# Issuing a small first load from ScalarE's queue, beside the first large load, in a DMA-bound pooling kernel

## The chip, the cores and the metric

The kernel runs on one core of one Trainium2 chip. The metric is the device time of one execution in microseconds (us); medians of several executions are quoted with their range. A trace also gives the span, from the first to the last recorded event, which is 1.8 us shorter than the time in most kernels here. "SP" and "ACT" are the two queues that issue transfers; both feed the same 16 DMA engines: in the trace of the kernel before, the packets of both (3,501 and 1,053) lie on the same 16 strings, one for each engine. ACT (ScalarE) and DVE (VectorE) also do the arithmetic. "Row" means the contiguous piece that one DMA engine moves as one packet into one partition (the 19 large loads into 128 partitions are 2,432 packets of 52,736 bytes).

## The reference

Average pooling with p = 2: squares are summed over windows of four, divided by four, and the square root is taken.

```python
x: (32, 256, 4096) float32, p = 2.0, kernel_size = 4
window = np.abs(x[:, :, 4*i : 4*i+4]) ** p
result[:, :, i] = np.mean(window, axis=-1) ** (1.0 / p)     # (32, 256, 1024)
```

So 134.22 MB are read and 33.55 MB written, with little arithmetic for each byte.

## The kernel before

The input is cut into 20 pieces of 128 partitions, most of them 13,184 columns wide (52,736 bytes in each partition), which go through three buffers. ACT squares a piece in place, DVE sums groups of four, ACT takes the root, and a store follows for every two pieces. 840 columns' worth of elements (430 KB) do not fit this pattern: the "odd" piece. It is viewed as 30 rows of 3,584 elements and borrows part of the second output buffer.

```python
def load(i):
    ...
    nc.sync.dma_start(out=v, in_=block(xf, g, 1)[:, src:src + w])
...
Q = 30
odd = ODD * P // Q                      # 3,584 elements
t = o_tiles[1][0:Q, 0:odd]
nc.sync.dma_start(out=t, in_=xf[(total - ODD) * P:total * P].rearrange("(p w) -> p w", p=Q))
ahead = 0
while ahead < n and loads[ahead][0] < X_SLOTS:      # three large loads at once
    load(ahead)
    ahead += 1
nc.vector.tensor_tensor(out=t, in0=t, in1=t, op=mybir.AluOpType.mult)
o = o_tiles[1][0:Q, odd:odd + odd // k]
nc.vector.tensor_reduce(out=o, in_=t.rearrange("p (n j) -> p n j", j=k), ...)
nc.scalar.activation(out=o, in_=o, func=Act.Sqrt, scale=1.0 / k)
stores["odd"] = nc.scalar.dma_start(out=of[...], in_=o)
for i in range(n):                      # the large pieces
    ...                                 # load(s) into a free buffer, Square, sum, root, store
```

## Time and profile before

| | before |
|---|---|
| median of the first three runs | 394.82 us (393.62 to 395.62) |
| span of the profiled run | 393.3 us |
| DVE, ACT busy | 70%, 70% |
| DMA engines, both queues | 99% |
| bytes moved | 167.77 MB at 427 GB/s |

The lines that carry this stand in the prediction. Two more views are needed. The first is the page's list of transfers: what is written from what, queue, operation and count, size of each, us from issue to landing.

```profile
xt<-in_x_dram SPq DMA_DIRECT2D x19, 6592.0 KB, 31.6
ot<-in_x_dram SPq DMA_DIRECT2D x1, 420.0 KB, 4.2
out_dram<-ot ACTq DMA_DIRECT2D x1, 105.0 KB, 8.7
```

The small load, alone at the start, lands after 4.2 us. The second is the timeline: the squares of the second and third large piece begin when these pieces have landed, within half a microsecond (start, duration, engine, line, operation, and in brackets the idle time and what ended it).

```profile
36.18 11.19 ACT L167 ACTIVATE xt<-xt 128x13184 f32<-128x13184 f32 x1 [4.39 <-DMA xt<-in_x_dram]
51.76 11.19 ACT L167 ACTIVATE xt<-xt 128x13184 f32<-128x13184 f32 x1 [4.39 <-DMA xt<-in_x_dram]
```

Third, a tool: the single packets of the trace. Each has a start, a duration, a queue and a size, but no engine number. Each large load ends with a 4-byte packet on each of its engines; the times of these 16 packets tell when the first, the middle and the last engine finished that load. In the kernel before, the third load was done at 50.73, 51.19 and 51.34 us; its 16 semaphore events follow 0.4 to 0.5 us later, from 51.13 to 51.82 on the same count. All packet times here, those of the prediction included, count from a moment some 0.08 us ahead of the zero of the timeline; differences between packets are not touched by that.

### The profile page before, as it was taken

Reading aid. Unit: us, or ns where it says so; the run is one execution under the profiler, and the core shown is the slowest. Engines: PE = TensorE matmul, PEld = TensorE weight load, DVE = VectorE, ACT = ScalarE, POOL = GpSimd, SP = SyncE. Lnnn points to the kernel's source line nnn. Section 1 sums busy time; section 2 is a strip of 40 time slices with the busy share of each in tenths; the row PEclk is TensorE's granted clock in tenths of the full one; section 3 lists DMA queues with packets and bytes.
Section 4 is the critical chain, followed back from the end, with each engine's and each line's share of the span. In section 5 each row is a group of like instructions: output and inputs, shape, how many; then the busy total and the mean of one; then the engine's idle time right before and its main releaser. Section 6 shows DMA issues by size and latency. Waiting matters only on the chain.

```text
span 393.3 us, 182 instructions
## 1 busy us (share of the span) xinstructions
DVE 274.5 (70%) x36; ACT 275.4 (70%) x38; POOL 0.2 (0%) x4
## 2 busy tenths in 40 slices
DVE  4207898885869376948693869396929690989991
ACT  1095879919990899099809991998099809986991
POOL 0000000000000000000000000000000000000000
DMA  8999999999989999999999999999999899999996
GB/s 312 429 440 429 467 445 451 381 432 469 434 386 429 472 429 429 456 402 429 429 432 426 429 472 429 456 400 467 429 437 429 386 429 467 429 429 423 440 409 295
DMA packets 4554, 167.77 MB, mean 427 GB/s; under 512 B 526, under 2 KB 526, under 8 KB 556
## 3 DMA queue, kind: packets, MB, share of 16 engines
q1 hardware_dynamic: 3501, 144.04, 85.0%
q10 hardware_dynamic: 1053, 23.73, 14.0%
HBM read 134.22 MB, written 33.55 MB: 427 GB/s over the span
## 4 chain that ended last, share of the span: by engine, by line
DMA 54%; ACT 25%; DVE 19%; SPq 0%; issue 0%; ACTq 0%
DMA xt<-in_x_dram 54%; ACT xt L167 22%; DVE ot L111 14%; DVE xt L122 3%; ACT ot L102 3%; DVE ot L124 1%; DVE xt L124 1%; ACT xt L102 1%; SPq L82 0%; ACTq L99 0%; SPq L132 0%
## 5 line engine op out<-in xcount | busy, mean ns | idle before, releaser
L167 ACT ACTIVATE xt<-xt 128x13184 f32<-128x13184 f32 (+4 forms) x23 | 217.4, 9458 | 97.9 <-DMA xt<-in_x_dram 96.2
L111 DVE TENSOR_REDUCE ot<-xt 128x3296 f32<-128x13184 f32 x15 | 208.3, 13886 | 88.7 <-ACT xt L167 88.7
L102 ACT ACTIVATE ot<-ot 128x6592 f32<-128x6592 f32 x9 | 51.1, 5679 | 0.0
L122 DVE TENSOR_TENSOR xt<-xt 128x3296 f32<-128x3296 f32 (+5 forms) x9 | 34.5, 3834 | 16.9 <-ACT xt L167 16.8
L124 DVE TENSOR_TENSOR ot<-xt 128x3296 f32<-128x3296 f32 (+1 forms) x4 | 10.9, 2733 | 0.1
L143 ACT ACTIVATE ot<-ot 30x896 f32<-30x896 f32 x1 | 0.9, 948 | 10.8 <-DVE ot L139 10.8
L137 DVE TENSOR_TENSOR ot<-ot 30x3584 f32<-30x3584 f32 x1 | 3.9, 3880 | 5.0 <-DMA ot<-in_x_dram 5.0
L124 DVE TENSOR_TENSOR xt<-xt 128x1448 f32<-128x1448 f32 (+4 forms) x5 | 7.0, 1409 | 0.2
L102 ACT ACTIVATE xt<-xt 128x3296 f32<-128x3296 f32 (+3 forms) x4 | 5.8, 1445 | 1.1 <-DVE xt L124 1.1
L164 DVE TENSOR_TENSOR xt<-xt 128x5792 f32<-128x5792 f32 x1 | 6.2, 6184 | 0.0
L139 DVE TENSOR_REDUCE ot<-ot 30x896 f32<-30x3584 f32 x1 | 3.9, 3874 | 0.0
L143 ACT ACT_TABLE_LOAD x1 | 1.3, 1283 | 0.7 <-PEq L200 0.7
L200 POOL MEMSET const-bfloat16-1.0<- 128x1 bf16 x1 | 0.1, 101 | 0.0
L200 POOL MEMSET const-uint8-127<- 128x1 uint8 x1 | 0.1, 101 | 0.0
L200 POOL MEMSET const-float32-0.0<- 128x1 f32 x1 | 0.1, 98 | 0.2 <-issue 0.2
L200 POOL MEMSET const-float32-1.0<- 128x1 f32 x1 | 0.1, 98 | 0.0
## 6 DMA issues: line engine op xcount, KB each, us to landing
xt<-in_x_dram SPq DMA_DIRECT2D x19, 6592.0 KB, 31.6
out_dram<-ot ACTq DMA_DIRECT2D x7, 3296.0 KB, 27.4
out_dram<-ot SPq DMA_DIRECT2D x2, 3296.0 KB, 24.0
xt<-in_x_dram SPq DMA_DIRECT2D x1, 5404.0 KB, 24.1
out_dram<-xt SPq DMA_DIRECT2D x1, 1648.0 KB, 11.0
out_dram<-xt SPq DMA_DIRECT2D x1, 1351.0 KB, 6.6
ot<-in_x_dram SPq DMA_DIRECT2D x1, 420.0 KB, 4.2
out_dram<-ot ACTq DMA_DIRECT2D x1, 105.0 KB, 8.7
```

What stands on the lines that cost most here:

```text
L102: r = nc.scalar.activation(out=o, in_=o, func=Act.Sqrt, scale=1.0 / k)
L111: r = nc.vector.tensor_reduce(out=o, in_=v.rearrange("p (n j) -> p n j", j=k), axis=mybir.AxisListType.X, op=add,)
L122: r = nc.vector.tensor_tensor(out=h, in0=q[:, :, 0:2], in1=q[:, :, 2:4], op=add)
L124: r = nc.vector.tensor_tensor(out=o, in0=h[:, :, 0], in1=h[:, :, 1], op=add)
L137: nc.vector.tensor_tensor(out=t, in0=t, in1=t, op=mybir.AluOpType.mult)
L139: nc.vector.tensor_reduce(out=o, in_=t.rearrange("p (n j) -> p n j", j=k), axis=mybir.AxisListType.X, op=mybir.AluOpType.add,)
L143: nc.scalar.activation(out=o, in_=o, func=Act.Sqrt, scale=1.0 / k)
L164: r = nc.vector.tensor_tensor(out=v, in0=v, in1=v, op=mybir.AluOpType.mult)
L167: r = nc.scalar.activation(out=v, in_=v, func=Act.Square)
L200: nc = _bacc.Bacc("TRN2", target_bir_lowering=False, num_devices=1)
```

## The change

SP takes about half a microsecond for the small load (an issue of 0.45 us and a gap of 0.06) before it issues the first large one at 1.24 us. The change gives the small issue to ACT's queue, so that both start at once. Nothing else moves.

```diff
-    nc.sync.dma_start(out=t, in_=xf[(total - ODD) * P:total * P].rearrange("(p w) -> p w", p=Q))
+    nc.scalar.dma_start(out=t, in_=xf[(total - ODD) * P:total * P].rearrange("(p w) -> p w", p=Q))
```

## The prediction

The sum: it came to -0.51 us at best and 0 at worst, taken as -0.3, so 394.82 - 0.3 = 394.5 us.

> **What bounds the kernel now.** I read the head of the page first, to see whether an engine or the transfers are full.
>
> ```profile
> DVE 274.5 (70%) x36; ACT 275.4 (70%) x38; POOL 0.2 (0%) x4
> DMA packets 4554, 167.77 MB, mean 427 GB/s; under 512 B 526, under 2 KB 526, under 8 KB 556
> q1 hardware_dynamic: 3501, 144.04, 85.0%
> q10 hardware_dynamic: 1053, 23.73, 14.0%
> DMA xt<-in_x_dram 54%; ACT xt L167 22%; DVE ot L111 14%; DVE xt L122 3%; ACT ot L102 3%; DVE ot L124 1%; DVE xt L124 1%; ACT xt L102 1%; SPq L82 0%; ACTq L99 0%; SPq L132 0%
> ```
>
> The two compute engines are busy 70%. The packets of the two queues take 85.0 + 14.0 = 99% of the time of the 16 DMA engines, so the kernel is bound by moving 167.77 MB. The chain that ended last (the last line) names compute for 46%, but that is a path through buffer releases: while ACT and DVE work, loads issued earlier keep the DMA engines full. A cheaper or earlier compute step is worth nothing unless it lets a DMA engine start earlier, end earlier, or not run dry.
>
> Second, the busy time by stretches, at the two ends and in the middle. Columns: stretch, its length, busy us of DVE, ACT and POOL with instruction counts, clock, DMA share, GB/s. (A packet is booked whole where it falls, so short stretches overshoot 1.)
>
> ```profile
> 0.00:1.00 1.00, 0.00 (x0) 0.27 (x1) 0.20 (x4) 1.00 0.00 0
> 1.00:2.00 1.00, 0.00 (x0) 1.00 (x1) 0.00 (x0) 1.00 0.70 186
> 60.00:360.00 300.00, 215.73 (x23) 218.58 (x26) 0.00 (x0) 1.00 1.00 434
> 388.00:390.00 2.00, 0.00 (x0) 0.00 (x0) 0.00 (x0) 1.00 1.01 428
> 390.00:392.00 2.00, 0.00 (x0) 0.00 (x0) 0.00 (x0) 1.00 0.14 59
> ```
>
> The middle runs at share 1.00 and 434 GB/s: nothing to win. The DMA is idle only in the first 2 us and the last 3. The change touches the first 2.
>
> Third, the timeline of the start.
>
> ```profile
> 0.73 1.28 ACT L143 ACT_TABLE_LOAD   x1 [0.73 <-PEq L200]
> 0.73 0.45 SPq L132 DMA_DIRECT2D ot<-in_x_dram  x1
> 1.24 44.83 SPq L82 DMA_DIRECT2D xt<-in_x_dram  x4
> 4.96 3.88 DVE L137 TENSOR_TENSOR ot<-ot 30x3584 f32<-30x3584 f32 x1 [4.96 <-DMA ot<-in_x_dram]
> 8.88 3.87 DVE L139 TENSOR_REDUCE ot<-ot 30x896 f32<-30x3584 f32 x1
> 12.78 0.95 ACT L143 ACTIVATE ot<-ot 30x896 f32<-30x896 f32 x1 [10.77 <-DVE ot L139]
> 13.76 0.64 ACTq L144 DMA_DIRECT2D out_dram<-ot  x1
> 20.60 11.19 ACT L167 ACTIVATE xt<-xt 128x13184 f32<-128x13184 f32 x1 [6.87 <-DMA xt<-in_x_dram]
> ```
>
> SP needs 0.45 us to issue the small load and starts the first large one at 1.24. That 1.24 - 0.73 = 0.51 us is all that the change can take off SP. The small piece is off the path: it is done at 14.40, while ACT's first square waits for the large load until 20.60.
>
> Fourth, I followed the single packets of the trace by engine (each packet starts some 3 ns before the one ahead of it on its engine ends, so 16 strings can be told apart). Fifteen of them carry two 14,336-byte rows of the small load, start at 1.81 to 2.34 us, and go on with a 52,736-byte row of the large load at 3.2 to 4.0 without a gap. The sixteenth has no part of the small piece: its first packet, a large row, starts at 2.94, which is 1.70 after SP began that issue. From then on no string shows a gap. At the end the fifteen finish at 390.3 to 390.7 and **the sixteenth at 392.17**, though it moved 35,848 bytes less. Four large-row stretches explain it: its rows normally take 1.947 us, but two near 70 us took 2.22 and 2.77, and four between 304 and 325 us took 2.18 to 2.37, some 2.3 us lost in all. So what sets the end in this execution is the one engine whose start the change can bring forward.
>
> [...] what can be saved is the 0.51 us above, and the strings are shared by both queues. [...] the trace shows 30 rows on 15 strings, two each. [...] the small store of 105 KB, issued on ACT's queue beside a running large load, takes 8.7 us to land, against 4.2 for the small load that goes first; its rows start at 17.59 to 20.03, after one or two large rows of 1.95 us each. [...]
>
> **The change part by part.**
> Removed: one issue of 0.45 us plus 0.06 gap from SP's queue, on the path to the first large packet. Effect if nothing takes its place: SP begins the large load at 0.73, the sixteenth engine's first packet at 0.73 + 1.70 = 2.43 instead of 2.94, and its end moves from 392.17 to 391.66: **-0.51 us**. It stays the last (the others end by 390.7 and move the same bytes).
> Added: one issue of about 0.45 us on ACT's queue at 0.73, ahead of the table load of 1.28 us. The table load then ends near 2.5; its first user is the square root of the small piece, not before 12.78. **Cost 0.**
> Moved: the small load now shares each of fifteen engines with a large load. These engines have the same bytes to move from the same earliest start (1.8), so their end does not change: **0**, perhaps plus 0.1 to 0.4 if their first packet comes later, still inside their slack of 392.17 - 390.7 = 1.5 us.
> Moved with it: the small piece's own chain. Taking the small store's 8.7 us as an estimate for a small transfer between large rows, it lands at 0.73 + 8.7 = 9.4 instead of 4.96. Then 3.88 + 3.87 on DVE and 0.95 on ACT, with some 0.1 of hand-over, end at 18.2, and the store's issue of 0.64 at 18.9. The first square comes at 20.60, so 1.7 us are left: **0**. Were it to overrun, the first square and through it the release of the first buffer would slip; the fourth large load goes out at 46.07 - 0.33 = 45.7, while the third's last rows end at 51.34, and with 1.7 us from issue to packet some 3.9 us are still to spare before an engine would run dry.
> The small store moves later by about 4.5 us, with the same bytes. The next user of that output buffer is the second pair's reduction after 60 us: 0.
> Sum: -0.51 us at best as worked out, 0 at worst that I think likely. I take half to most of it: **-0.3**, so 394.82 - 0.3 = 394.5.
>
> **The rivals.** (a) *The full half microsecond*: both issues run side by side at 0.73 and the sixteenth engine is the last again. For it: the end of the strings. It gives 394.3. [...] (c) *The last engine is another one*: the six long rows of the sixteenth engine may be accidents of that execution. Without them it would end at about 389.9, ahead of the fifteen, and then a start half a microsecond earlier buys nothing: 394.8. For it: the long rows come in two clusters. Against: all other engines have only one or none beyond their first row, and it is unlikely that chance picks just the one engine without a small piece. (d) *Harm by taking turns*: the small piece lands so late behind large rows that ACT[...] begins the first square late, and the buffer release with it. It needs a landing later than 11.1 us to touch the square and later than about 15 to starve an engine; that would make 395.5 to 398. Two large rows ahead of each of its two rows would be 4 x 1.95 = 7.8 us after 2, so 9.8: against it. (e) *More than half a microsecond*: the first rows are slow (the first large rows take 2.3 to 2.8 us instead of 1.95, the small ones 0.6 to 1.1 against the 0.53 that 14,336 bytes take at the large rows' rate). Beginning both together might hide some of this; up to 1 us, 393.8.
>
> **Range and chances.** The mechanism spans 393.8 to 394.8 with a tail to 396. The three times of the kernel before spread over 2.0 us (393.62 to 395.62), larger than the effect; a median of three on each side moves by some 0.7 us. Together about 1.2 us either way for 8 in 10: **393.3 to 395.7 around 394.5**. Two per cent is 7.9 us; the idle DMA time at both ends is only some 5 us together, so faster by over 2% is all but impossible (0.005), and slower by over 2% needs an engine to run dry several times (0.01). Within 2%: 0.985.
>
> **What would show it.** Right: in the timeline SP's first large issue starts at 0.73 and ACT's small one too, each of 0.35 to 0.5 us; the sixteenth string's first packet is near 2.43; the small piece's DVE work starts between 7 and 10 us; the first square still at 20.0 to 20.7; DMA share 1.00 in the middle; the whole ends 0.3 to 0.5 us earlier, with the sixteenth string last. [...] Rival (c): another string is last. Wrong altogether: the first square later than 21.5, a gap in the strings near 50 us, a new wait in the list of waits that names a store or a small load, or a middle stretch under 430 GB/s.

## The result

| | before | changed |
|---|---|---|
| median of 6 runs each, same rounds | 394.45 us (393.62 to 395.62) | 395.91 us (395.55 to 396.20) |
| ratio | | 1.0032, 95% interval 1.0011 to 1.0053 |
| span of the profiled run | 393.3 us | 394.0 us |

A ratio in this document compares two kernels in the same rounds; it stays within 0.0003 of the ratio of their mean times and is not quite that of the medians quoted. The change is within 2%, as predicted, but it made the kernel slower by 0.3%, and 395.91 lies above the predicted range (393.3 to 395.7).

The page of the changed kernel, same lines as in the prediction (engines, packets, the two queues, the chain that ended last):

```profile
DVE 274.5 (70%) x36; ACT 275.4 (70%) x38; POOL 0.2 (0%) x4
DMA packets 4554, 167.77 MB, mean 426 GB/s; under 512 B 526, under 2 KB 526, under 8 KB 556
q1 hardware_dynamic: 3456, 143.61, 84.9%
q10 hardware_dynamic: 1098, 24.16, 14.3%
DMA xt<-in_x_dram 50%; ACT xt L167 25%; DVE ot L111 14%; DVE xt L122 3%; ACT ot L102 3%; DVE ot L124 1%; DVE xt L124 1%; ACT xt L102 1%; ACTq L99 0%; SPq L82 0%
```

The 45 packets and 0.43 MB of the small load have moved from SP's queue (q1) to ACT's (q10). Work, bytes and packets are the same, and so is the share of 99% (85.0 + 14.0 before, 84.9 + 14.3 now). So the engines were not idle longer; they took longer for the same bytes. The timeline says when:

```profile
0.73 95.70 SPq L82 DMA_DIRECT2D xt<-in_x_dram  x7
0.74 0.65 ACTq L132 DMA_DIRECT2D ot<-in_x_dram  x1
1.42 1.28 ACT L143 ACT_TABLE_LOAD   x1 [1.42 <-PEq L200]
12.57 3.88 DVE L137 TENSOR_TENSOR ot<-ot 30x3584 f32<-30x3584 f32 x1 [12.57 <-DMA ot<-in_x_dram]
20.39 0.95 ACT L143 ACTIVATE ot<-ot 30x896 f32<-30x896 f32 x1 [17.69 <-DVE ot L139]
22.31 11.19 ACT L167 ACTIVATE xt<-xt 128x13184 f32<-128x13184 f32 x1 [0.97 <-DMA xt<-in_x_dram]
38.16 11.19 ACT L167 ACTIVATE xt<-xt 128x13184 f32<-128x13184 f32 x1 [4.66 <-DMA xt<-in_x_dram]
53.75 11.19 ACT L167 ACTIVATE xt<-xt 128x13184 f32<-128x13184 f32 x1 [4.40 <-DMA xt<-in_x_dram]
```

The first square starts at 22.31 instead of 20.60, the third at 53.75 instead of 51.76. Each was released by the large load, not by the small piece, whose root was done at 21.34. The loss of 2 us is complete by the time the second square starts. The rates of the first 10 us agree (stretch, length, busy time of DVE, ACT, POOL, clock, DMA share, GB/s; a packet is booked whole, so such short stretches are rough). Before:

```profile
2.00:12.00 10.00, 7.00 (x2) 0.01 (x1) 0.00 (x0) 1.00 1.10 436
```

Changed:

```profile
2.00:12.00 10.00, 0.00 (x0) 0.70 (x1) 0.00 (x0) 1.00 0.91 307
```

The packets say what was slow. A row of 52,736 bytes normally takes 1.947 us. In the kernel before, 17 such rows that start in the first 16 us take over 2.1 us: the first large row of each engine, and a second one on one engine. In the changed kernel it is 48, the first three of each of the 16 engines, at 2.2 to 3.6 us, while the small rows pass between them. One of these engines has no small row at all, and its rows are as slow (2.65, 2.90 and 2.89 us). Per engine:

| mean over the engines, us lost against full rate | before | changed |
|---|---|---|
| large rows of the first 16 us, over 1.947 us each | 0.55 | 2.31 |
| two small rows, over the 0.53 us that 14,336 bytes take at that rate | 2 x (0.87 - 0.53) = 0.68 | 2 x (0.73 - 0.53) = 0.40 |
| sum | 1.23 | 2.71 |
| third load done on the middle engine | 51.19 us | 52.65 us |

The sums differ by 1.48 us, the landings of the third load by 1.46. So the start accounts for the delay of the middle engine, and that delay lasts: 1.36 us at 301 us, where a later load lands on the middle engine at 300.44 before and 301.80 changed. The two spans differ by only 0.7 us because in the trace of before one engine loses another 1.3 us on four slow rows after 304 us and ends 1.5 us behind the others.

### The profile page after: what moved, and what is told of

Its sections match the earlier page's. It is cut to its first block, busy times and chain, and to the rows that moved or that the text cites. A ratio compares the mean times of both kernels' runs of the same rounds, so it can differ in the third digit from the quotient of the medians.

```text
span 394.0 us, 182 instructions
## 1 busy us (share of the span) xinstructions
DVE 274.5 (70%) x36; ACT 275.4 (70%) x38; POOL 0.2 (0%) x4
## 3 DMA queue, kind: packets, MB, share of 16 engines
q1 hardware_dynamic: 3456, 143.61, 84.9%
q10 hardware_dynamic: 1098, 24.16, 14.3%
## 4 chain that ended last, share of the span: by engine, by line
DMA 50%; ACT 28%; DVE 19%; another core or an unknown queue 1%; issue 0%; ACTq 0%; SPq 0%
DMA xt<-in_x_dram 50%; ACT xt L167 25%; DVE ot L111 14%; DVE xt L122 3%; ACT ot L102 3%; DVE ot L124 1%; DVE xt L124 1%; ACT xt L102 1%; ACTq L99 0%; SPq L82 0%
## 6 DMA issues: line engine op xcount, KB each, us to landing
ot<-in_x_dram ACTq DMA_DIRECT2D x1, 420.0 KB, 11.8
```

## The experiments

Two theories were on the table first. **Turns:** an engine that alternates between two queues which both load loses time at each turn. **Start:** the engines are slow for their first 10 us, whatever comes. A third came with them. **Place:** the 30 rows go to partitions 0 to 29, the large rows to all 128; what counts is to which partitions the small rows are written. "Crowding" below is short for the slow large rows (2.2 to 3.6 us in the changed kernel) that go with small rows in the low partitions. This theory stood as a guess until the runs below. The prediction had counted the engines that take part (15), and had not asked to which partitions they write.

All kernels gave right results unless it is said otherwise. Medians of before differ between the sets of runs (394.06, 393.92, 395.00, 394.55 us), so the ratios are what compares. The runs came in four sets, each on one chip, with before in the same rounds. The times of before fall into two groups, about 393.7 to 394.1 and 394.9 to 395.5 us, and the share of the slower group differs: it is 8 of 11 runs in the set of the 60-row versions and 4 or 2 of 11 in the two sets ahead of it, which makes the ratios of the 60-row versions look better. In the versions that move the root behind the first square, or compute the small piece in two halves, the time exceeds the span by some 2.0 us (2.6 in act_later) instead of 1.8, so some 0.2 us of their loss lies outside the traced work.

### One queue, the large load first

```diff
-    small load on nc.sync, then load(0), load(1), load(2)
+    load(0) on nc.sync, small load on nc.sync, then load(1), load(2)
     # the small piece's root and store: behind the first Square on ACT
```

> The small load goes back to SP's queue, but behind the first large load; its square root moves behind the first square on ACT, so that nothing waits for it. One queue, the large load first. Turn theory (each turn between two queues that both load costs time on the engine, whenever it happens): no turns, so the first large rows show no run of 2.7 us rows beyond the very first, the first square starts at 19.0 to 19.7 us (20.60 before, less 0.5 us of issue and about 1 us of small rows that now come after), and the time is that of before less 0.3 to 0.5 us, about 1.3 to 2 us under the changed kernel. Start theory (the engines are slow in their first 10 us whatever comes): the second and third large rows take 2.7 us here too, the first square comes near 21.5 to 22, and the time is near 395.5. Place theory[...]: the small rows take about 0.9 us each and slow their neighbours here as well; time like before or up to 1 us over it.

Measured: 396.08 us (395.63 to 396.67), ratio 1.0047 (1.0030 to 1.0064). Nearly all rows run at 1.95 us from the second on, so the start theory falls. But from 18 us, where the small rows pass, the next large rows take 2.1 to 3.5 us, most of them 2.6 to 3.1, with no second load queue anywhere; the 3.49 us are on the engine that has no small row. The turn theory, which expected no such rows and a gain, falls for this loss as well. The third load is done at 51.27, 52.32 and 53.18 (first, middle, last engine). The stretch in which the small rows pass:

```profile
16.00:26.00 10.00, 3.60 (x1) 5.72 (x1) 0.00 (x0) 1.00 1.03 375
```

### ACT's queue, later

```diff
+    for _ in range(2):
+        nc.vector.memset(o_tiles[1][:, :], 0.0)     # the load must wait for these
     nc.scalar.dma_start(out=t, in_=...)             # root behind the first Square
```

> The small load stays on ACT's queue, but waits for two fills of its buffer on DVE, so that it is issued some 7 to 16 us in, when the large rows run at 1.95 us each; its root comes behind the first square. Turn theory: each of the fifteen engines again has about two large rows of 2.4 to 2.9 us around its two small rows, the third square starts 1.3 to 2 us later than in a kernel without turns (about 52.5 to 53.5), and the time is that of the changed kernel, near 395.9. Start theory: no row above 2.1 us around the small ones, the third square near 51.3, the time 0.3 to 0.5 under before. Place theory: in between, the small rows slow (0.9) and the large beside them somewhat.

Measured: 397.52 us (397.18 to 398.72), ratio 1.0090 (1.0070 to 1.0109); its time exceeds its span by 2.6 us instead of 1.8, so part of this lies outside the traced work. The load was issued at 14.75 us. Full speed ahead of the small rows, slow large rows beside them (means of 2.4 to 2.9 us between 18 and 26 us): the cost goes where the small rows go. Stretch of the run with the late load:

```profile
12.00:16.00 4.00, 2.72 (x1) 0.57 (x1) 0.00 (x0) 1.00 0.98 422
16.00:26.00 10.00, 0.00 (x0) 5.57 (x2) 0.00 (x0) 1.00 1.10 370
26.00:60.00 34.00, 31.42 (x4) 25.22 (x5) 0.00 (x0) 1.00 0.99 427
```

The rate falls to 370 GB/s only in the middle line, in which the small rows pass.

### Two large loads on two queues

```diff
-        nc.sync.dma_start(out=v, in_=...)
+        (nc.scalar if i == 1 else nc.sync).dma_start(out=v, in_=...)
```

> The kernel before with the second large load issued from ACT's queue, so that two queues with equal 52,736-byte rows alternate for 128 rows each. Its time is not the point: the first square must come near 36 us and the engines may run dry near 51 us. Turn theory: each row takes 2.4 to 2.9 us while both queues load, the rate from 8 to 35 us falls to 300 to 360 GB/s. Start theory: slow only until about 11 us, then 1.95 us a row and about 430 GB/s. Place theory: no slow rows after the small piece has landed, about 430 GB/s.

Measured: one run of unknown state, 409.20 us; the fourth large load was issued only at 62.38 us, so the engines ran dry near 50 us, as foreseen, and only the rows count.

```profile
2.00:8.00 6.00, 0.00 (x0) 0.45 (x1) 0.00 (x0) 1.00 1.01 324
8.00:35.00 27.00, 7.75 (x2) 0.95 (x1) 0.00 (x0) 1.00 1.02 440
```

From 8 to 35 us two queues load side by side at 440 GB/s, with rows of 1.95 us. Alternation as such cost nothing here: the turn theory is out.

### 128 small rows on ACT's queue

```diff
-    Q = 30
+    Q = 128
```

> The changed kernel with the small piece as 128 rows of 3,360 bytes in place of 30 rows of 14,336: eight rows on each of sixteen engines. Turn theory: up to eight turns per engine in place of two, so the slow stretch lasts four times as long: large rows of 2.4 to 2.9 us until about 25 us, the small piece lands after 20 us, and the time is 398 to 401. Start theory: slow rows only until about 11 us as in the changed kernel, time near 395.9. Place theory: rows go to all 128 partitions, no crowding, large rows at 1.95 from the second on, first square near 20.6, time near 394.

Measured: 395.48 us (395.27 to 396.18), ratio 1.0032 (1.0014 to 1.0050). The turns became four times as many, yet large rows run at 1.947 us from the second on, and the small rows take 0.13 us. Place expected this; the time, however, is not the 394 that it expected. The small piece landed late (DVE began it at 20.68) and its root held up the first square to 23.61, and most of the remaining loss comes later, as told below (0.99 us per engine near 70 us).

### The same 64 rows in two places

```diff
-    Q = 30;  t = o_tiles[1][0:Q, 0:odd]
+    Q, P0 = 64, 0        # act_64_low: partitions 0 to 63
+    Q, P0 = 64, 32       # act_64_mid: partitions 32 to 95
+    t = o_tiles[1][P0:P0 + Q, 0:odd]     # computed in two halves of 32; root behind the first Square
```

With 64 rows all 16 engines take part: q10 has 1,168 packets in both, 70 more than in the changed kernel, which are 34 rows and one 4-byte packet more in the small load and as many in the small store. The trace does not show which engine writes where; what the expectations here and for the 60 rows took for granted about it is cut. Between the two runs everything but the place is the same, the bytes read included.

> After the first runs two equal load queues alternate at full speed, and 128 small rows on ACT's queue slowed no large row, so the place where the small rows land is the suspect. Here the small piece is 64 rows of 6,720 bytes on ACT's queue at the start, in partitions 0 to 63, its root behind the first square. Place theory: [...] large rows of 2.4 to 2.9 us appear between the small ones until about 10 to 12 us, and the small rows take more than the 0.25 us that 6,720 bytes need; third square 53 to 54, time 395.5 to 396.5. Rival, shape theory (what counts is how long the small rows are, or that only fifteen engines take part): no slow large rows beyond the first, third square 51.5 to 52.

> The same 64 rows, the same two instructions for each step, the same queue and order, only in partitions 32 to 95 instead of 0 to 63[...]. Place theory: small rows about 0.26 us each, no large row above 2.1 us after the first, third square 51.5 to 52, 1 to 2 us ahead of the run with partitions 0 to 63. Shape theory: no difference between the two.

Measured, in the same rounds on one chip: low 396.55 us (396.13 to 397.27), ratio 1.0062 (1.0044 to 1.0080); mid 395.24 us (394.64 to 395.75), ratio 1.0026 (1.0006 to 1.0047). The means of the four runs each, 396.62 and 395.22, differ by 1.4 us. Rates of the first 16 us and start of the third square, low:

```profile
2.00:16.00 14.00, 0.00 (x0) 0.61 (x1) 0.00 (x0) 1.00 0.97 358
```

```profile
53.50 11.19 ACT L171 ACTIVATE xt<-xt 128x13184 f32<-128x13184 f32 x1 [4.64 <-DMA xt<-in_x_dram]
```

Mid:

```profile
2.00:16.00 14.00, 0.00 (x0) 0.67 (x1) 0.00 (x0) 1.00 0.95 404
```

```profile
52.03 11.19 ACT L171 ACTIVATE xt<-xt 128x13184 f32<-128x13184 f32 x1 [4.64 <-DMA xt<-in_x_dram]
```

The third square comes 1.47 us apart. In low, 78 large rows of the first 16 us take over 2.1 us (means of 2.33 to 2.41 us from 6 to 16 us); in mid 16, the first of each engine. **The place of the small rows decides.** What the runs show is the dependence on the partitions, not how it comes about. In low all 16 engines have slow rows, and in the changed kernel, with 30 rows, the engine that has no small row is slowed like the rest (2.65, 2.90 and 2.89 us). How the delay reaches that engine is open. The 30 rows themselves were not moved; that their loss is of the same kind is argued from the same slow rows.

### Without the crowding, other orders

```diff
 second_128:  one_queue_second with Q = 128
 sp_128:      before with Q = 128
 act_60_mid:  changed kernel with 60 rows in partitions 32 to 91, root behind the first Square
 sp_60_mid:   before with 60 rows in partitions 32 to 91
```

> One queue, large load first, small piece second as 128 rows of 3,360 bytes over all partitions, root behind the first square. Place theory: only the first large row is slow (about 2.6), small rows 0.13, no slow large row after them; first square 19.5 to 19.8, third near 51.2, and a time 1.5 to 2.5 us under the same order with 30 rows (396.08), so 393.6 to 394.6, level with or a little under before (394.06). If the 30-row shape is not what costs, it stays near 396.

> The kernel before with the small piece as 128 rows over all partitions, first on SP's queue. It tells what the place costs when the small piece goes first. Place theory: the small rows take 0.13 us instead of 0.87 for four times the size, so the first large rows start about 0.7 us earlier than before (2.9 instead of 3.2 to 4.0), but the first large rows still pay the cold start (about 2.6); the third square comes 0 to 0.8 us earlier than 51.76, the time is 0 to 0.8 us under before. Against: the engine without a share before now has one, which costs it 1.1 us and may leave the end where it was.

> The change made without crowding: the small load on ACT's queue at the start, as 60 rows in partitions 32 to 91, [...] the engine that starts last has no share. Root behind the first square. Place theory: no slow large row but the first, the third load on the last engine at 51.2 to 51.7, time 1 to 2 us under the changed kernel, 393.7 to 394.8: the half microsecond hoped for from the change is then at most what is left against before. If it stays at 395.5 or more, place is not the whole loss.

> The kernel before with the same 60 rows in partitions 32 to 91, small load first on SP's queue. Place theory: the small rows take about 0.27 us, done on each engine about 0.7 us sooner than the two of 0.87 before, the first large rows may start sooner; the last engine starts late but has 1.3 us less to move. Third load on the last engine at 50.7 to 51.3, time 393.2 to 394.2, that is up to 0.7 us under before. If the start of the large rows is bound by when SP's second issue takes effect (2.9 us in the trace of before), the gain is only 0 to 0.3.

| | time, us | ratio to before (95%) | third load done: first, middle, last engine |
|---|---|---|---|
| before (first trace) | | | 50.73, 51.19, 51.34 |
| changed (first trace) | 395.91 | 1.0032 (1.0011 to 1.0053) | 51.45, 52.65, 53.34 |
| second_128 | 395.26 | 1.0030 (1.0017 to 1.0044) | 50.57, 50.86, 51.77 |
| sp_128 | 395.16 | 1.0023 (1.0009 to 1.0037) | 50.35, 50.70, 52.04 |
| act_60_mid | 394.74 | 1.0007 (0.9989 to 1.0025) | 49.57, 50.69, 51.40 |
| sp_60_mid | 395.38 | 1.0013 (0.9995 to 1.0031) | 50.29, 50.53, 50.72 |

At the third load the place theory did well: without crowding the middle engine is 0.3 to 0.7 us ahead of before instead of 1.46 us behind. Its times were missed in three of the four cases (that of act_60_mid was met): by the ratios nothing ends sooner than before. As times, the intervals of the changed kernel and of act_60_mid overlap, and the two did not share rounds, so only the third load tells them apart. Two things can be read from the packets. In sp_128 the last engine is 1.34 us behind the middle one (52.04 against 50.70), and before it is 0.15: one engine begins its first large row later than the rest (4.13 us against 3.49 for the fifteenth), and with 128 rows it also has a share of the small piece. Keeping a share from the late starter is not assured by using fifteen engines, though: in the changed kernel and in act_60_mid the engine that starts last (at 3.16 and 2.62 us) does have small rows, against the expectation.

The 60-row versions lose their lead near 70 us: in sp_60_mid the middle engine is 0.70 us ahead of before at the fourth load (66.08 against 66.78) and 0.37 us behind at 145 us. Large rows that start between 67.5 and 74.6 us lose 1.30 us per engine there, 1.04 in act_60_mid, 0.6 to 1.0 in act_64_mid and the 128-row versions, 0.21 and 0.23 in the two traces of before and 0.01 in both of the changed kernel. The first large store is issued just ahead of these rows (at 67.85 us in sp_60_mid, 68.50 in act_60_mid, 68.56 before). The other versions that crowd the start lose almost nothing here either (0.01 in act_64_low and one_queue_second, 0.05 in act_later): part of what is saved at the start is lost at the first store. Why is open.

### Second traces of both kernels

> The kernel before once more, for a second trace. Its times fall into two groups (about 393.7 to 394.1, and 394.9 to 395.5), and the first trace is one of the slower group: one engine lost about 1.3 us on four rows between 304 and 325 us. If that is the difference of the groups, a trace of the fast group has no such engine at the end: the last packet ends near 391 instead of 392.17, and the third load has landed on all engines near 51.3 again. If the groups come from the start, the third load lands 1 us earlier or later than 51.34.

> The changed kernel once more. If what it loses is the crowding at the start, this trace shows again three slow large rows (2.3 to 3 us) on each engine in the first 11 us, the third load landed on the last engine near 53.3, some 2 us after 51.34 of before, and a time of 395.5 to 396.2. If the slow rows were an accident of one execution they are missing here.

Measured, one run each of unknown state: before 395.03, changed 395.30 us. The slow rows come back: 16 over 2.1 us before, 48 changed; the third load is done on the last engine at 51.33 and 53.03 us. The loss per engine at the start of the changed kernel is smaller this time: 1.83 us on large rows and 2 x (0.69 - 0.53) = 0.32 on small ones, 0.92 us over the 1.23 of before, and its middle landing is 52.15, 0.96 over 51.19. The time of 395.30 is accordingly lower than in the first six runs, and under the expected 395.5.

The run of before fell into the slower of its two groups of times again, and again one engine ended 1.5 us after all others (392.07 against 390.56 us). It is not the engine of the first trace: the one without a small row ends at 390.56 with the others. The slow rows of this trace after the start are at 70, 72, 149, 158, 161 and 228 us. Without that engine the span would be some 1.5 us shorter, 391.7, near the spans of the faster group (391.9 to 392.3). That fits, but no trace of the faster group was taken, so it is not shown.

### A pause ahead of the first large store

```diff
+        if g == 0:
+            nc.scalar.activation(out=pause, in_=pause, func=Act.Square)   # then the store
```

> The 60-row version on SP's queue, with one more square (of data that nobody reads again) on ACT ahead of the first large store, which so is issued about 1.7 us later. If the loss comes with the start of the store itself, slow large rows appear again, 1.7 us later (near 71.5 to 76 us), the same 1 us is lost between the fourth load and 145 us, and the time stays 395.0 to 395.5. If it depends on where the store meets the load stream, the slow rows are gone or fewer, and the time is 393.5 to 394.5.

> The same pause in the version with 60 rows on ACT's queue. Store itself: slow rows near 72 to 76, time as without the pause, 394.4 to 395.0. Meeting point: gone or fewer, time 393.3 to 394.2, which would be under the kernel before.

> The same pause in the kernel before. Store itself: nothing changes beyond 0.2 us. Meeting point: its few slow rows near 70 us vanish and with them part of the lag of one engine: time as the faster group of its executions, 393.5 to 394.2, fewer in the slower group.

These three gave wrong results: the piece of buffer that the pause squares is by then receiving the sums of the third large load. For the same reason the pause waited for that sum and the store came out at 76.5 to 76.9 us, some 8 us late instead of 1.7. The times are 395.60 us (394.49 to 396.26), 396.35 (396.29 to 396.74) and 396.15 (394.34 to 396.24), and can't be set beside the others. The traces still say one thing: the slow rows moved with the store. In sp_60_mid_pause none is left near 70 us, and rows of 2.2 to 3.3 us start between 77.8 and 81.5, after a store issued at 76.53. So the loss near 70 us goes with the start of the first large store. (In before_pause, 16 rows of 2.3 to 2.6 us also start between 85 and 87.4 us; no cause was found.) Why it costs 0.01 us in one kernel and 1.3 in another stays open.

## Why the prediction was wrong

**What bounds the kernel: right.** The changed kernel is bound by the 16 DMA engines (84.9 + 14.3 = 99% of their time), and compute did not matter: the small piece's chain ended at 21.34 us, ahead of the first square at 22.31.

**Removed, -0.51 us: the start came true, the end did not.** SP's first large issue began at 0.73. The engine that was to profit, the one without a small row, started at 2.09 us in the first trace and 2.04 in the second, against 2.94 and 2.89 before: 0.85 us earlier, more than forecast. (The 1.70 us of the prediction mix two clocks and are 1.62 on one.) But its first three large rows lost 2.6 us instead of 1.1, and it finished the third load at 51.45, 0.72 us later than before. And that this engine sets the end held in one execution only: in the second trace of before another engine does, by 1.5 us.

**Added, 0: right.** The table load moved from 0.73 to 1.42 and delayed nothing.

**Moved, 0: this is the step that failed.** "These engines have the same bytes to move from the same earliest start (1.8), so their end does not change" takes for granted that an engine needs the same time for the same bytes in any order. Here it did not: with the small rows in partitions 0 to 29 passing between them, the large rows lost 2.31 instead of 0.55 us per engine. When the small load goes first, each engine is done with its small rows before its first large row; they take 0.87 instead of 0.53 us then, and the loss is 1.23 us in all instead of 2.71. Corrected for this term, the sum is +1.0 to +1.5 us at the middle engine in the two traces, against +1.26 us by the ratio of times (0.32% of 394.45).

**The small chain: mis-sized, harmless.** The small load took 11.8 us to land, not 8.7. The estimate was drawn from a small store, whose rows of 3,584 bytes took 0.14 us each and slowed no large row. Its margin of 1.7 us would have been overrun had the large load not been late as well. A first square later than 21.5 us, which the prediction named as the sign of being wrong altogether, came at 22.31.

**The rivals.** Rival (d), harm by taking turns, named the right range (395.5 to 398) but a wrong path: the first square was late because of the large load, not because of the small one. Rivals (a) and (e) are out by the time. Of the two issues side by side, SP's took 0.38 us, against 0.36 for the same issue before; ACT's took 0.65 instead of the 0.45 assumed (an issue of the small store with nothing beside it took 0.64 before, so this shows no wait). Rival (c), that the long rows of the sixteenth engine were an accident, is borne out for the kernel before by its second trace; it foresaw no gain, but no loss either.

**The spread.** The two groups of before's times were taken as noise around one value. The changed kernel's first six runs lie within 0.65 us, so the interval of the ratio excludes 1 although the effect is only 1.3 us.

## What to carry to other kernels

Before two transfers are put side by side on a kernel that is bound by its DMA engines, ask to which partitions each of them writes. Here 30 rows in partitions 0 to 29 and 64 rows in 0 to 63 slowed the large rows of all engines, whichever queue they came from; 64 rows in 32 to 95, 60 in 32 to 91 and 128 over all partitions did not. Of the places in time tried for the 30 rows, alone at the start, as in the kernel before, was the cheapest. No version tried here beat the kernel before; the placed one on ACT's queue is level with it (1.0007, 0.9989 to 1.0025). A better start need not give a better time: part of what was won there was lost again at the first large store.

Two more things that the packets show may be looked for elsewhere. An engine's first large row took longer than the 1.947 us of the later ones: 2.43 us on the mean behind the 30 small rows of the kernel before, 2.5 to 2.7 where it came first, but only 2.06 to 2.10 behind small rows in other places (sp_60_mid, sp_128). And one engine started later than the others: in the changed kernel its first large row began at 3.16 us, those of the other fifteen at 1.82 to 2.13.
